# A two-layer decoder: first projections accumulated tile by tile, wide modulation rows moved into the first feed-forward

## The chip, the core and the metric

The kernel runs on one core of one Trainium2 chip. The core has TensorE (PE, matrix products), VectorE (DVE), ScalarE (ACT), GpSimd (POOL) and SyncE (SP), which here issues the loads and stores, and 16 DMA engines. The metric is the device time of one execution in microseconds (us), median of several runs. Lower is better.

## The reference

The reference is a decoder trunk of two layers for 1024 tokens of width 1024. A small vector `cond = silu(c)` is multiplied with a 1024 x 6144 matrix in each layer; the six parts of the result (48 columns of 128, called modulation) shift, scale and gate the two sub-layers.

```python
cond = jax.nn.silu(c)
for l in range(DEPTH):                                  # 2
    mod = cond @ w_mod[l] + b_mod[l]
    sh1, sc1, gt1, sh2, sc2, gt2 = [m[:, None, :] for m in jnp.split(mod, N_MOD, axis=-1)]
    h = rms_norm(x, norm_g[l, 0]) * (1.0 + sc1) + sh1
    y = mixer_block(h, positions, w_in[l], ...)         # conv | sparse attention | linear attention | gMLP, then w_o
    x = x + gt1 * rms_norm(y, norm_g[l, 1])
    h = rms_norm(x, norm_g[l, 2]) * (1.0 + sc2) + sh2
    y = jnp.square(jax.nn.relu(h @ w_up[l])) @ w_down[l]
    x = x + gt2 * rms_norm(y, norm_g[l, 3])
```

## The kernel before, in words

Activations lie transposed: a tile is 128 features x 512 tokens, eight tiles make 1024 features. The tokens go in two halves, `hf` 0 and 1. The program runs `mods_start`, then `mix(0,0)`, `mix(0,1)`, `ff(0,0)`, `mix(1,0)`, `ff(0,1)`, `mix(1,1)`, `ff(1,0)`, `ff(1,1)`. A scheduler that runs when the program is built interleaves them on each engine's queue, which is then fixed; between engines semaphores hold the order.

A product of float precision is made of three matmuls (`mm3`, L166 to L169): high part by high, high by low, low by high. So a GEMM for one 128-wide chunk of output (`gemm`, L171) is 8 tiles x 3 = 24 matmuls of 128x512. Its weights come in two halves of 256 KB: SP loads `raw_a` (L152), ScalarE casts the high part (L161), VectorE subtracts to get the low part (`sub`, L125). Lanes a, b and f are three sets of such weight buffers: a for the first and last projections of a mixer, b for the projections of linear attention, gMLP and convolution, f for the feed-forward. `h` tiles are made by `make_h` from x, the reciprocal norm R, the scale A1 and the shift, again as a high and a low part (two VectorE operations, L134, and one ScalarE operation, L203, for each tile).

A modulation column (`mod_col`, L228) takes 128 outputs: two loads of a 128x512 row of weights (256 KB each), for each a VectorE multiply with a sum along the row (L232, followed by a short read of the accumulator), and one short operation that adds the two sums and the bias. `mods_start` (L248) makes the columns of the first shift and scale, 32 rows named `mw`, in twelve buffers, together with the reciprocal norm; the h tiles follow. The other 80 columns, 160 rows named `mr`, have two buffers in the pool `work` (`mods`, L271). They are written in the program after the convolution of `mix(0,0)` (parts 2 to 4 of layer 0) and after `mix(0,1)` (part 5 of layer 0, all of layer 1), and the scheduler puts them between other VectorE work from early on.

In `mix(0,0)` the chunk for the gates (10) and the five for sparse attention (17 to 21) are projected first, each in a PSUM bank of the tag mm. Rotary tables (`rope_tables`) are made by VectorE from the positions, transposed and spread by small matmuls, copied by ScalarE, written to memory (`cosd`, `sind`) and read back as `cs`; GpSimd multiplies q and k with them. Then come key compression (L650), attention (L744 on), linear attention, gMLP and convolution, and the four groups' outputs are normalised, split (L216 on ScalarE, L125 on VectorE) and projected by `w_o` in lane a.

## Time and profile before

| | us |
|---|---|
| median of 3 runs | 2655.94 |
| lowest, highest | 2654.65, 2660.86 |
| span of the profiled execution | 2656.2 |
| TensorE busy in it | 2513.5 |
| VectorE busy in it | 1680.0 |
| ScalarE busy in it | 1310.3 |

The profile is of one execution; its span is within 0.3 us of the median of the runs. A busy time counts an engine's instructions from start to end; matmuls overlap, so the pitch from one start to the next tells more than a duration. The granted clock is a share of TensorE's full clock; its two levels here are 1.0 (2.4 GHz) and 0.5 (1.2 GHz). The rows that are read stand two sections below.

### The profile page before, as it was taken

To read this page: it belongs to the slowest core of one execution; us is meant where nothing else is said; L and a number is where in the kernel's file an instruction comes from. 1 tells how busy PE (TensorE), PEld (TensorE's weight loads), DVE (VectorE), ACT (ScalarE), POOL (GpSimd) and SP (SyncE) were. 2 spreads that over 40 slices of the span, in tenths; PEclk is the share of its full clock that TensorE was granted. 3 is DMA by queue.
4 is the path that set the end of the run, shared out by engine and by line. 5 is a ranking of instruction groups with operands and counts; after the bars stand their busy time and mean duration, and the time that the engine had idled before them with its cause. 6 is when DMAs were issued, how large, how long until landed. Compare 5 with 4: busy or idle time off the path is not lost.

```text
span 2656.2 us, 34273 instructions
## 1 busy us (share of the span) xinstructions
PE 2513.5 (95%) x11690; PEld 1989.3 (75%) x11690; DVE 1680.0 (63%) x3540; ACT 1310.3 (49%) x2649; POOL 56.5 (2%) x65
## 2 busy tenths in 40 slices
PE   2899879999999999999999999999999999999998
PEld 1676657677778887767788887777777888788887
DVE  7797987888574448457674446547876544534446
ACT  3474534468654345356653435345775443434343
POOL 0100000200000000010000000001000000000000
PEclk9999989999999999999999999999999999999999
DMA  7435566511343334222243334222123333533332
GB/s 270 138 97 174 192 204 202 179 53 36 100 142 98 96 99 143 82 71 69 95 144 100 96 97 145 88 61 89 40 76 121 98 96 99 179 97 98 96 99 84
DMA packets 168937, 301.56 MB, mean 114 GB/s; under 512 B 20453, under 2 KB 24122, under 8 KB 168762
## 3 DMA queue, kind: packets, MB, share of 16 engines
q1 hardware_dynamic: 168762, 299.37, 36.3%
q8 instruction: 92, 1.51, 0.2%
q14 instruction: 83, 0.68, 0.1%
HBM read 281.47 MB, written 17.83 MB: 113 GB/s over the span
## 4 chain that ended last, share of the span: by engine, by line
PE 76%; DVE 10%; ACT 4%; DMA 4%; issue 2%; POOL 0%; DVEq 0%; SPq 0%; ACTq 0%; POOLq 0%
PE ps_ff L168 16%; PE ps_ff L169 16%; PE ps_ff L167 16%; PE ps_mm L167 6%; PE ps_mm L169 6%; PE ps_mm L168 6%; DMA mr<-in_w_mod_dram 3%; PE ps_pv L705 1%; PE ps_pv L704 1%; DVE mr L232 1%; PE ps_mm L699 1%; ACT bp L754 1%; PE ps_t L189 1%; PE ps_s L744 1%; DVE w_a L125 1%
## 5 line engine op out<-in xcount | busy, mean ns | idle before, releaser
L161 ACT CAST w_f<-raw_f 128x512 fp32r<-128x512 f32 x504 | 313.3, 622 | 649.7 <-PE ps_ff L168 638.6
L125 DVE TENSOR_TENSOR w_f<-raw_f,w_f 128x512 fp32r<-128x512 f32 x504 | 348.7, 692 | 261.6 <-ACT w_f L161 254.7
L169 PE MATMUL ps_ff<-h,w_f 128*128 128x512 f32 x1024 | 405.9, 397 | 17.1 <-DVE w_f L125 17.1
L167 PE MATMUL ps_ff<-h,w_f 128*128 128x512 f32 x1024 | 404.8, 396 | 4.8 <-ACT h L203 4.8
L168 PE MATMUL ps_ff<-h,w_f 128*128 128x512 f32 x1024 | 406.6, 397 | 0.6 <-DVE h L134 0.4
L167 PE MATMUL ps_ff<-hid,w_f 128*128 128x512 f32 x992 | 388.9, 392 | 0.1
L168 PE MATMUL ps_ff<-hid,w_f 128*128 128x512 f32 x992 | 388.6, 392 | 0.0
L169 PE MATMUL ps_ff<-hid,w_f 128*128 128x512 f32 x992 | 388.2, 391 | 0.0
L167 PE MATMUL ps_mm<-h,w_a 128*128 128x512 f32 x832 | 336.4, 405 | 34.8 <-ACT w_a L161 30.5
L169 PE MATMUL ps_mm<-h,w_a 128*128 128x512 f32 x832 | 332.7, 400 | 11.7 <-DVE w_a L125 11.6
L168 PE MATMUL ps_mm<-h,w_a 128*128 128x512 f32 x832 | 338.8, 409 | 0.9 <-DVE h L125 0.9
L131 DVE TENSOR_TENSOR y<-y,ps_ff 128x512 f32<-128x512 f32 (+1 forms) x232 | 154.9, 668 | 238.0 <-PE ps_ff L169 237.1
L161 ACT CAST w_a<-raw_a 128x512 fp32r<-128x512 f32 x208 | 128.6, 618 | 233.0 <-PE ps_mm L168 216.2
L169 PEld LDWEIGHTS ps_ff<-h,w_f 128*128 128x128 f32 x1024 | 195.0, 190 | 60.1 <-DVE w_f L125 18.8
L125 DVE TENSOR_TENSOR w_a<-raw_a,w_a 128x512 fp32r<-128x512 f32 x208 | 143.3, 689 | 152.2 <-ACT w_a L161 146.0
L167 PEld LDWEIGHTS ps_ff<-h,w_f 128*128 128x128 f32 x1024 | 195.4, 191 | 47.6 <-ACT h L203 6.5
L168 PEld LDWEIGHTS ps_ff<-h,w_f 128*128 128x128 f32 x1024 | 195.0, 190 | 45.2 <-issue 2.7
L167 PEld LDWEIGHTS ps_mm<-h,w_a 128*128 128x128 f32 x832 | 158.0, 190 | 81.2 <-ACT w_a L161 33.6
L167 PEld LDWEIGHTS ps_ff<-hid,w_f 128*128 128x128 f32 x992 | 186.6, 188 | 40.5 <-issue 1.4
L168 PEld LDWEIGHTS ps_ff<-hid,w_f 128*128 128x128 f32 x992 | 186.7, 188 | 39.1 <-issue 1.0
L169 PEld LDWEIGHTS ps_ff<-hid,w_f 128*128 128x128 f32 x992 | 186.7, 188 | 37.8 <-issue 0.5
L169 PEld LDWEIGHTS ps_mm<-h,w_a 128*128 128x128 f32 x832 | 157.9, 190 | 55.8 <-DVE w_a L125 15.1
(350 smaller groups left out, 3586.4 us busy)
## 6 DMA issues: line engine op xcount, KB each, us to landing
raw_f<-in_w_up_dram SPq DMA_DIRECT2D x256, 256.0 KB, 2.7
raw_f<-in_w_down_dram SPq DMA_DIRECT2D x256, 256.0 KB, 2.6
mr<-in_w_mod_dram SPq DMA_DIRECT2D x160, 256.0 KB, 3.0
raw_a<-in_w_in_dram SPq DMA_DIRECT2D x144, 256.0 KB, 2.8
raw_a<-in_w_o_dram SPq DMA_DIRECT2D x64, 256.0 KB, 2.9
mw<-in_w_mod_dram SPq DMA_DIRECT2D x32, 256.0 KB, 4.4
bp<-in_cmp_w_dram SPq DMA_DIRECT2D x32, 256.0 KB, 4.6
raw_b<-in_w_in_dram SPq DMA_DIRECT2D x32, 256.0 KB, 3.0
```

Source lines behind the costliest of these rows:

```text
L125: V.tensor_tensor(out=out, in0=a, in1=b, op=ALU.subtract)
L131: eng.tensor_tensor(out=out, in0=a, in1=b, op=ALU.add)
L161: A.copy(hi, raw)
L167: PE.matmul(ps_ap, wh, xh, start=start, stop=False)
L168: PE.matmul(ps_ap, wh, xl, start=False, stop=False)
L169: PE.matmul(ps_ap, wl, xh, start=False, stop=stop)
L189: PE.matmul(p, ones, acc, start=True, stop=True)
L232: V.tensor_tensor_reduce(out=raw, in0=raw, in1=cond[kh], scale=1.0, scalar=0.0, op0=ALU.mult, op1=ALU.add, accum_out=mp[:, kh:kh + 1])
L699: PE.transpose(tp[0:kn, hh, :], cols(h0 + hh), ident)
L704: PE.matmul(pv[:, h0:h0 + nh, :], vst, th[0:kn], start=first[0], stop=False)
L705: PE.matmul(pv[:, h0:h0 + nh, :], vst, tl[0:kn], start=False, stop=last)
L744: PE.matmul(sp[:, 0:w], qh[:, h0 + hh, :], KX[:, 128 * k0:128 * k0 + w], start=True, stop=False)
```

## The change

`cond` becomes one tile of 1024, and a modulation row is 1024 wide: one load of 512 KB and one VectorE operation for a column instead of two. The start makes columns, h tiles and the six chunks' GEMMs together: after tile k of h, each of the six chunks gets its three matmuls of that tile, in six PSUM banks (two each of the tags mm, ff and s); their weights are loaded and split for four tiles at a time, at k = 0 and k = 4. `gate_part` and `nsa_part` take these banks as they are. The modulation of parts 2 to 4 of layer 0 (24 rows) runs after the convolution with three buffers in the place of the convolution's tiles. Part 5 of layer 0 and all of layer 1 but one part (48 rows) are handed out one row for each down-projection unit of `ff(0,0)`, with two buffers; the last part (8 rows) in `ff(0,1)`. The table matmuls of `rope_tables` move from the tag s to the single bank of the tag t.

```diff
-    def mod_col(l, j, k, mk):
-        mp = work.tile([128, 2], F32, name="mp", tag="mp", bufs=4)
-        for kh in range(2):
-            raw = mk(w_mod[l, 8 * j + k, :, kh * T:kh * T + T], [128, T])
-            V.tensor_tensor_reduce(out=raw, in0=raw, in1=cond[kh], scale=1.0, scalar=0.0,
-                                   op0=ALU.mult, op1=ALU.add, accum_out=mp[:, kh:kh + 1])
-        stt(par[l]["mod"][:, j, k:k + 1], mp[:, 0:1], mp[:, 1:2], par[l]["bmod"][:, 8 * j + k:8 * j + k + 1],
-            ALU.add, ALU.add)
+    def mod_dot(l, j, k, mk, acc):
+        raw = mk(w_mod[l, 8 * j + k], [128, 1024])
+        V.tensor_tensor_reduce(out=raw, in0=raw, in1=cond, scale=1.0, scalar=0.0,
+                               op0=ALU.mult, op1=ALU.add, accum_out=acc)
...
-    def mods_start():
-        with region("su") as su:
+    EARLY = (10, 17, 18, 19, 20, 21)
+
+    def start():
+        d = par[0]
+        early = {}
+        with region("kw", "right") as kw, region("su") as su:
             def mk(src, shape):
-                t = su.tile(shape, F32, name="mw", tag="mw", bufs=12)
+                t = su.tile(shape, F32, name="mw", tag="mw", bufs=5)
                 dma(out=t, in_=src)
                 return t
+
+            def wload(n, kh):
+                raw = kw.tile([128, 4, 128], F32, name="raw_k", tag="raw_k", bufs=6)
+                dma(out=raw, in_=w_in[0, n, :, 4 * kh:4 * kh + 4, :])
+                return raw
+
+            def wsplit(raw):
+                hi, lo = (kw.tile([128, 4, 128], F32R, name="w_k", tag="w_k", bufs=12) for _ in range(2))
+                A.copy(hi, raw)
+                sub(lo, raw, hi.bitcast(F32))
+                return hi, lo
...
             for k in range(8):
+                ma = work.tile([128, 2, 1], F32, name="ma", tag="ma", bufs=4)
                 for j in (0, 1):
-                    mod_col(0, j, k, mk)
+                    mod_dot(0, j, k, mk, ma[:, j, :])
+                add(d["mod"][:, 0:2, k:k + 1], ma, bm[:, 0:2, k:k + 1])
                 mod_scale(0, 1, slice(k, k + 1))
+                if k % 4 == 0:
+                    raws = [wload(n, k // 4) for n in EARLY]
+                h = make_h(xt, R, d["A1"], d["mod"][:, 0, :], (k,))
+                hs = h if k == 0 else hs + h
+                if k % 4 == 0:
+                    ws = {n: wsplit(r) for n, r in zip(EARLY, raws)}
+                for i, n in enumerate(EARLY):
+                    if k == 0:
+                        early[n] = ps(("mm", "mm", "ff", "ff", "s", "s")[i])
+                    hi, lo = ws[n]
+                    mm3(early[n], hi[:, k % 4, :], lo[:, k % 4, :], hs[k][0], hs[k][1], k == 0, k == 7)
...
-    def mods(l, js):
+    def mods(l, j, pl, bufs):
 
         def mk(src, shape):
-            t = work.tile(shape, F32, name="mr", tag="mr", bufs=2)
+            t = pl.tile(shape, F32, name="mr", tag="mr", bufs=bufs)
...
+        ma = work.tile([128, 8], F32, name="mv", tag="mv", bufs=2)
+        for k in range(8):
+            mod_dot(l, j, k, mk, ma[:, k:k + 1])
+            if k == 7:
+                add(par[l]["mod"][:, j, :], ma, par[l]["bmod"][:, 8 * j:8 * j + 8])
+                mod_scale(l, j, slice(0, 8))
+            yield
...
                 for w, dst in ((0, cosd), (128, sind)):
-                    p = ps("s")
+                    p = ps("t")
...
-                    mods(0, (2, 3, 4))
+                    with region("md", "right") as rg:
+                        for _ in mods_all(((0, 2), (0, 3), (0, 4)), rg, 3):
+                            pass
...
+                next(filler, None)
                 for k in range(G):
...
-    mods(0, (5,))
-    mods(1, range(6))
-    xt = ff(0, 0)
+    xt = ff(0, 0, ((0, 5), (1, 1), (1, 0), (1, 2), (1, 4), (1, 3)))
...
-    xt = ff(0, 1)
+    xt = ff(0, 1, ((1, 5),))
```

On TensorE, the first matmuls of the program in the kernel before (`ps_mm_417` is the bank of chunk 10, `h_346` and `h_347` the high and low part of the first h tile, `h_352` and `h_353` the second's):

```order
L189 MATMUL ps_t_194<-nt_171,ones_71 128x512
L167 MATMUL ps_mm_417<-h_346,w_a_420 128x512
L168 MATMUL ps_mm_417<-h_347,w_a_420 128x512
L169 MATMUL ps_mm_417<-h_346,w_a_422 128x512
L167 MATMUL ps_mm_417<-h_352,w_a_420 128x512
L168 MATMUL ps_mm_417<-h_353,w_a_420 128x512
```

And of the change, the end of the first h tile's round and the begin of the second's (`h_224`, `h_225` are the first tile's parts, `h_287`, `h_288` the second's):

```order
L167 MATMUL ps_s_272<-h_224,w_k_248 128x512
L168 MATMUL ps_s_272<-h_224,w_k_248 128x512
L169 MATMUL ps_s_272<-h_224,w_k_249 128x512
L167 MATMUL ps_mm_252<-h_287,w_k_228 128x512
L167 MATMUL ps_mm_256<-h_287,w_k_232 128x512
L167 MATMUL ps_ff_260<-h_287,w_k_236 128x512
L167 MATMUL ps_ff_264<-h_287,w_k_240 128x512
L167 MATMUL ps_s_268<-h_287,w_k_244 128x512
L168 MATMUL ps_mm_252<-h_288,w_k_228 128x512
L169 MATMUL ps_mm_252<-h_287,w_k_229 128x512
```

Before, one chunk ran through all eight tiles in one bank; now all six banks take a tile's matmuls before the next tile.

On VectorE, where the normalised outputs of `mix(0,0)` are split for the output projection (`of_2341` and `of_2463` are the convolution's outputs), the kernel before:

```order
L134 SCALAR_TENSOR_TENSOR of_2341<-of_2341,gain0_99,nt_2512 128x512
L134 SCALAR_TENSOR_TENSOR of_2463<-of_2463,gain0_99,nt_2512 128x512
L131 TENSOR_TENSOR nt_2717<-nt_2717,nt_2719 128x512
L125 TENSOR_TENSOR h_2730<-of_2341,h_2729 128x512
L134 SCALAR_TENSOR_TENSOR mod0_100<-mp_6417,bmod0_96 128x1
L125 TENSOR_TENSOR h_2734<-of_2463,h_2733 128x512
L232 ISA mr_6426,mp_6425<-mr_6426,cond0_125 128x512
L232 ISA mp_6425 128x1
L125 TENSOR_TENSOR h_2738<-of_2160,h_2737 128x512
L232 ISA mr_6429,mp_6425<-mr_6429,cond1_126 128x512
```

The same place in the change (`of_2280` and `of_2402` are the convolution's outputs):

```order
L134 SCALAR_TENSOR_TENSOR of_2280<-of_2280,gain0_99,nt_2451 128x512
L134 SCALAR_TENSOR_TENSOR of_2402<-of_2402,gain0_99,nt_2451 128x512
L232 ISA mr_2471,mv_2461<-mr_2471,cond_125 128x1024
L232 ISA mv_2461 128x1
L232 ISA mr_2474,mv_2461<-mr_2474,cond_125 128x1024
L232 ISA mv_2461 128x1
L232 ISA mr_2477,mv_2461<-mr_2477,cond_125 128x1024
L232 ISA mv_2461 128x1
L131 TENSOR_TENSOR nt_2546<-nt_2546,nt_2548 128x512
L125 TENSOR_TENSOR h_2559<-of_2280,h_2558 128x512
L232 ISA mr_2480,mv_2461<-mr_2480,cond_125 128x1024
L232 ISA mv_2461 128x1
```

Between the convolution's last operation and the projection's fifth weight split 23 of the 24 wide rows of parts 2 to 4 now stand, 17 of them ahead of the last split of the outputs; before, six narrow rows stood there.

On SP, loads in `ff(0,0)` in the change (before, this stretch holds `raw_f` loads and those of `w_o` and x alone):

```order
L305 DMA mr_6525<-in_w_mod_dram 128x1024
L305 DMA mr_6549<-in_w_mod_dram 128x1024
L152 DMA raw_f_7386<-in_w_up_dram 128x512
L152 DMA raw_f_7404<-in_w_up_dram 128x512
L410 DMA bg_9470<-in_gmlp_b_dram 64x128
L305 DMA mr_6573<-in_w_mod_dram 128x1024
L305 DMA mr_6597<-in_w_mod_dram 128x1024
L152 DMA raw_f_7430<-in_w_up_dram 128x512
L152 DMA raw_f_7448<-in_w_up_dram 128x512
L305 DMA mr_6800<-in_w_mod_dram 128x1024
```

Wide rows and weight halves alternate in one queue.

## Rows read from the trace of the kernel before

**Rows 1.** From the page, part 1: busy us (share of the span) and instructions.

```profile
PE 2513.5 (95%) x11690; PEld 1989.3 (75%) x11690; DVE 1680.0 (63%) x3540; ACT 1310.3 (49%) x2649; POOL 56.5 (2%) x65
```

**Rows 2.** Table of windows: span, busy us of each engine, clock, DMA share, GB/s.

```profile
25.00:50.00 25.00, 1.02 (x3) 0.79 (x3) 24.50 (x73) 5.56 (x8) 0.00 (x0) 1.00 0.66 212
100.00:275.00 175.00, 164.84 (x882) 122.91 (x879) 151.32 (x455) 97.44 (x249) 4.75 (x8) 0.98 0.41 126
350.00:375.00 25.00, 16.93 (x45) 10.84 (x45) 22.72 (x51) 10.64 (x17) 0.00 (x0) 0.78 0.54 168
400.00:550.00 150.00, 137.28 (x724) 102.61 (x723) 122.49 (x310) 64.67 (x135) 13.86 (x13) 0.99 0.56 176
850.00:950.00 100.00, 100.00 (x443) 82.84 (x442) 41.71 (x63) 41.04 (x68) 0.00 (x0) 1.00 0.34 98
1020.00:1350.00 330.00, 318.71 (x1538) 246.91 (x1537) 211.65 (x466) 181.49 (x399) 12.55 (x13) 0.97 0.28 88
```

**Rows 3.** Timeline of VectorE, start to 49 us: start, duration, engine, line, operation.

```profile
14.12 0.68 DVE L232 CUSTOM_DVE_ANT_0 mw<-mw,cond 128x512 f32<-128x512 f32 x1
...
40.06 0.68 DVE L232 CUSTOM_DVE_ANT_0 mw<-mw,cond 128x512 f32<-128x512 f32 x1
40.67 0.08 DVE L232 DVE_READ_ACCUMULATOR2_ANT mp<- 128x1 f32 x1
...
47.48 1.41 DVE L134 SCALAR_TENSOR_TENSOR h<-nt,mod,h 128x512 fp32r<-128x512 f32 x2
```

**Rows 4.** Timeline of TensorE, first six GEMMs.

```profile
50.42 0.63 PE L167 MATMUL ps_mm<-h,w_a 128*128 128x512 f32 x1
50.85 0.63 PE L168 MATMUL ps_mm<-h,w_a 128*128 128x512 f32 x1
...
54.10 0.39 PE L167 MATMUL ps_mm<-h,w_a 128*128 128x512 f32 x1
54.33 0.39 PE L168 MATMUL ps_mm<-h,w_a 128*128 128x512 f32 x1
...
93.39 0.40 PE L169 MATMUL ps_mm<-h,w_a 128*128 128x512 f32 x1
```

**Rows 5.** Timeline of TensorE, ScalarE and GpSimd, rotary tables to first attention.

```profile
60.25 0.60 PE L322 MATMUL ps_t<-ident,sc 128*17 128x128 f32 x4
...
67.11 0.59 ACT L329 COPY o<-ps_s 128x512 f32<-128x512 f32 x1 [0.27 <-PE ps_s L327]
...
75.97 2.56 POOL L128 TENSOR_TENSOR p<-p,cs 128x512 f32<-128x512 f32 x2 [72.89 <-DMA raw_b<-in_w_in_dram]
...
96.04 1.50 POOL L128 TENSOR_TENSOR p<-p,cs 128x512 f32<-128x512 f32 x1
...
109.14 0.33 PE L744 MATMUL ps_s<-KS,qh 128*128 128x128 f32 x1
```

**Rows 6.** Answer for the tile mr (160 modulation rows 512 wide).

```profile
L275 SPq DMA_DIRECT2D mr<-in_w_mod_dram x160: 327/328/1397, 73.6 to 540.7; - x160
L232 DVE CUSTOM_DVE_ANT_0 mr<-mr,cond x160: 647/686/1200, 82.2 to 544.5; 128x512 f32<-128x512 f32 x160
...
  DMA mr<-in_w_mod_dram: 36.6, 49
...
DMA to landing us min/median/max: 2.4/3.0/5.7
```

**Rows 7.** TensorE, convolution's end to output projection: timeline.

```profile
272.24 0.39 PE L169 MATMUL ps_mm<-h,w_b 128*128 128x512 f32 x1
...
281.46 0.80 PE L167 MATMUL ps_mm<-h,w_a 128*128 128x512 f32 x1 [3.36 <-ACT h L216]
```

**Rows 8.** Groups of instructions by line, 272 to 290 us.

```profile
L167 PE MATMUL ps_mm<-h,w_a 128*128 128x512 f32 x7 | 3.5, 502 | 3.6 <-ACT h L216 3.4 <-ACT w_a L161 0.3
L168 PE MATMUL ps_mm<-h,w_a 128*128 128x512 f32 x5 | 3.3, 664 | 0.9 <-DVE h L125 0.9
L169 PE MATMUL ps_mm<-h,w_a 128*128 128x512 f32 x5 | 2.4, 482 | 0.0
```

More of the change, by code (lines that the diff above doesn't have):

```diff
@@ L195, in rstd, with make_h @@
         return R
-    def make_h(xt, R, Ac, shc):
+    def make_h(xt, R, Ac, shc, ks=range(8)):
         h = []
-        for k in range(8):
+        for k in ks:
             t = nt()
@@ L244, in mod_scale @@
             mul(d["G1" if j == 2 else "G2"][:, ks], m, d["ng"][:, 1 if j == 2 else 3, ks])
-    cond = [const.tile([128, T], F32, name=f"cond{hf}") for hf in range(2)]
-    def mods_start():
-        with region("su") as su:
+    EARLY = (10, 17, 18, 19, 20, 21)
[3 more added lines that the diff above has]
+        with region("kw", "right") as kw, region("su") as su:
             def mk(src, shape):
-                t = su.tile(shape, F32, name="mw", tag="mw", bufs=12)
+                t = su.tile(shape, F32, name="mw", tag="mw", bufs=5)
                 dma(out=t, in_=src)
                 return t
+            def wload(n, kh):
[7 more added lines that the diff above has]
+                return hi, lo
             for hf in range(2):
+                cs = slice(hf * T, hf * T + T)
                 t1, t2 = (su.tile([128, T], F32, name="ct", tag="ct", bufs=4) for _ in range(2))
-                dma(out=cond[hf], in_=c[:, hf * T:hf * T + T].to_broadcast([128, T]))
-                logsig(t2, cond[hf], t1)
+                dma(out=cond[:, cs], in_=c[:, cs].to_broadcast([128, T]))
+                logsig(t2, cond[:, cs], t1)
                 A.activation(t2, t2, AF.Exp)
-                mul(cond[hf], cond[hf], t2)
+                mul(cond[:, cs], cond[:, cs], t2)
             xt = load_x(0)
@@ L410, in gmlp_part, with gate_part @@
         return group_out(y, st_[1], d["gain"][:, 6:8])
-    def gate_part(l, hf, h, gr, rg, lane):
-        p = ps("mm")
-        gemm(p, lane, w_in[l, GLA0], h)
+    def gate_part(l, hf, h, gr, rg, lane, early={}):
+        p = early.get(GLA0)
+        if p is None:
+            p = ps("mm")
+            gemm(p, lane, w_in[l, GLA0], h)
         lrT = rg.tile([32, T], F32, name="lrT")
@@ L566, in gla_part, with nsa_part @@
         return group_out(y, st_[1], d["gain"][:, 4:6])
-    def nsa_part(l, hf, h, rg, gates):
+    def nsa_part(l, hf, h, rg, gates, early={}):
         d = par[l]
@@ L581, in inproj @@
         def inproj(k):
-            p = ps("mm")
-            gemm(p, "a", w_in[l, NSA0 + k], h)
+            p = early.get(NSA0 + k)
+            if p is None:
+                p = ps("mm")
+                gemm(p, "a", w_in[l, NSA0 + k], h)
             return p
@@ L826, in ytile, with norm, mix @@
         return work.tile([128, T], F32, name="y", tag="y", bufs=8)
-    def norm(l, hf, xt, R=None):
+    def norm(l, hf, xt):
         d = par[l]
-        if R is None:
-            R = rms_R(xt, 1.0 / 1024)
+        R = rms_R(xt, 1.0 / 1024)
         return make_h(xt, R, d["A1"], d["mod"][:, 0, :])
-    def mix(l, hf, h, between=None):
+    def mix(l, hf, h, between=None, early={}):
         d = par[l]
@@ L842, in mix @@
                     with region("gl", "right") as rg:
[L843 removed]
+                        gates, lrT = gate_part(l, hf, h, gr, rg, "a", early)
                         rope_tables()
[L845 removed]
+                        yn = nsa_part(l, hf, h, es.enter_context(region("ns")), gates, early)
                         ol = gla_part(l, hf, h, rg, "b", sx, lrT)
@@ L881, in mix, with ff, ff_body @@
         return res
-    def ff(l, hf):
+    def ff(l, hf, todo=()):
+        with region("md") as rg:
+            return ff_body(l, hf, mods_all(todo, rg, 2))
+    def ff_body(l, hf, filler):
         d = par[l]
@@ L959, in load_x @@
         return xt
-    xt, R0 = mods_start()
-    h = norm(0, 0, xt, R0)
+    h, early = start()
     xt = load_x(1)
-    h = mix(0, 0, h, lambda: norm(0, 1, xt))
+    h = mix(0, 0, h, lambda: norm(0, 1, xt), early)
     mix(0, 1, h)
-    mods(0, (5,))
-    mods(1, range(6))
-    xt = ff(0, 0)
+    xt = ff(0, 0, ((0, 5), (1, 1), (1, 0), (1, 2), (1, 4), (1, 3)))
     h = norm(1, 0, xt)
     mix(1, 0, h)
-    xt = ff(0, 1)
+    xt = ff(0, 1, ((1, 5),))
     h = norm(1, 1, xt)
```

14 lines of the change are left out of this document (7 added, 7 removed).

## The prediction

> **What bounds the kernel now.** I read the page first. TensorE is busy 95% of the span, VectorE 63%, ScalarE 49% [rows 1]. So the span is the matmuls plus the places where TensorE waits or runs at half clock, and only those places can move. The table of windows shows where they are [rows 2]. From 25 to 50 us TensorE works 1.02 us while VectorE works 24.50 of 25: VectorE sets the start. From 100 to 275 TensorE is idle 10.2 us, from 350 to 375 it is idle 8.1 us at a mean granted clock of 0.78, from 400 to 550 it is idle 12.7 us. In a feed-forward stretch (850 to 950) it is idle 0 us, with VectorE at 41.7% and the DMA engines at 34%. From 1020 to 1350, where layer 1's first mixer is interleaved with feed-forward work and no modulation runs, it is idle 11.3 us in 330.
>
> The timeline then tells what the start is made of. VectorE runs the 32 modulation rows from 14.12 to 40.7 at a pitch of 0.61 us (40.06 to 40.67), with the h tiles among and after them; the last h is done at 48.89 [rows 3]. TensorE starts its first six GEMMs (144 matmuls) at 48.98, at half clock (0.43 us each, 50.42 to 50.85) and at full clock (0.23 us each) from 54.10 [rows 4]. They end at 93.8 [rows 4], and rotary tables, gates and weight splits all run underneath.
>
> **The start, part by part.** The change feeds the same 144 matmuls tile by tile, so they run under VectorE's work. VectorE's own list changes thus: 16 rows of 1024 at an estimated 1.15 us (a 512 row's 0.61 twice would be 1.22; one fixed part falls away) instead of 32 x 0.61: 18.4 for 19.5, -1.1; 8 short adds instead of 16, about -1; 12 weight subtracts put ahead of the end, at the same pitch since they have the same 128x512 shape, 12 x 0.61 = +7.3. So the last h comes about 5 us later, near 54, and the last 18 matmuls (4.1 us) end near 59. TensorE has 18 x 0.23 = 4.1 us of work for each 4.7 us of VectorE, so it never holds VectorE up. The DMA adds 3 MB of weights to a stretch with a third of its time free [rows 2]: no cost taken, at most 3 us. Alone this is 93.8 - 59 = 35 us of lead.
>
> Most of that lead can't be used. In the order of the change, the next long work on TensorE (compression, attention, the first lane-b GEMM) stands behind the rotary tables, and these no longer have GEMMs to hide under: the position load stands in SP's queue behind the loads of the second half's x, which wait for the start's last scratch tile; the gates' transposes stand behind all 144 matmuls; the table sines come after the gates on VectorE; and four table matmuls now share one PSUM bank. Before, the first table transpose ran at 60.25 and the last table copy ended at 67.70, 7.5 us [rows 5]. Now the transposes can start near 61, and the one bank makes the same steps take about 9: 70. Written to memory and read back, two transfers of 2.4 to 3.0 us [rows 6]: 76. That is just where GpSimd's first rotary multiply ran before, at 75.97 [rows 5]. But before, GpSimd's last multiply began at 96.04, because it waited for q's GEMMs; now all inputs are there, and six multiplies of 1.28 to 1.50 take 8.5 us: end near 84.5 instead of 97.5. The first attention matmul followed that end by 11.6 us (97.5 to 109.14 [rows 5]): compression adds, 64 compression matmuls. So it comes at 96: **-13 us**. Bounds: -25 if TensorE finds enough lane-b work to move ahead, -3 if the tables take 10 us longer.
>
> **The rows of (0,2) to (0,4).** Before, 160 rows of 512 wide sat between other VectorE work from 82 to 545 us, and VectorE stood still before 49 of them for 36.6 us on their transfers [rows 6]. 48 of these leave the stretch from 100 to 272; TensorE's idle time there, 10.2 us, mostly waits for softmax steps. Taken: **-4**, bounds 0 and -10.
>
> They come back as 24 wide rows between the convolution and the output projection. There TensorE's last convolution matmul starts at 272.24, the first of the output projection at 281.46, and in 272 to 290 only 7 + 5 + 5 = 17 GEMM matmuls run, 3.9 us of work at full clock: 14 us lost already [rows 7, 8]. VectorE now has 17 of the 24 rows before the last split of the normalised outputs, and SP issues the fifth weight half of the projection behind the 23rd row's load, which waits for a free buffer. By VectorE's own list: 24 x 1.15 + about 24 other operations x 0.61 = 42 us. By the three buffers: (1.15 + 0.33 for the issue + landing) / 3 for each row. A transfer of 256 KB lands in 2.4 to 5.7 us, 3.0 at the median [rows 6]; 512 KB is not in the trace. I take the second half at 0.7 to 1 us on top, so 3.1 to 6.5, likeliest 4, since the median is the nearest row: 1.83 x 24 = 44 us. Meanwhile TensorE has two and a half GEMMs, 60 matmuls, 13.6 us. Loss 28 to 30 instead of 14: **+14**. Bounds: +10, if the first rows start under the last GEMM; +35 at a landing of 6.5.
>
> The Trainium skill prices such a load on "DMA: Bandwidth & Descriptors", section "Anatomy of one DMA", at about 2.0 us plus bytes over 436 GB/s, measured on GpSimd's queue: 2.6 us for 256 KB, near the 3.0 here, and an estimate of 3.2 for 512 KB. By it the buffers would not bind, the sum would be some 5 us lower, and the rows in the feed-forward below would be free.
>
> **The other 56 columns.** Their 112 narrow rows leave 275 to 545. In 350 to 375 idle time and half clock cost about 12 us, in which 10 rows ran; I take **-8** (bounds -4, -12). In 400 to 550 the idle 12.7 us would be 5.1 at the rate of 1020 to 1350 [rows 2], so **-8** (bounds -3, -12). The wait near 343 stays: VectorE's row there is residual work.
>
> 48 of them run as wide rows inside ff(0,0), the last 8 in ff(0,1). A unit of 12 matmuls lasts 2.73 us; VectorE's work for it is one subtract, one add and a row, 0.61 + 0.61 + 1.15 = 2.37. It fits, but with two buffers a row can come only every (1.15 + 0.33 + landing) / 2: 2.74 us at a landing of 4. That is the unit's own pace. VectorE, waiting for a row, has the next weight subtracts queued behind it, and SP, waiting for a buffer, has the next weights. What softens it: the rows come in groups of eight with up-projections between, and weights are a few units ahead. Taken: **+3**, bounds 0 and +25.
>
> **Sum.** -13 - 4 + 14 - 8 - 8 + 3 = -16 against the span of 2656.2, which is 0.3 us from the median of the runs: **2640 us**.
>
> **The rivals.**
> *More of the lead kept* (2.5 in 10). TensorE takes lane-b GEMMs, output-projection work or the second half's norm while the tables are made, and the rows' loads land in 3 us: -25 - 6 + 10 - 10 - 10 + 0 = -41, 2615. For: transfers of 256 KB landed in 2.4 at best. Against: the order places the first lane-b GEMM behind attention's first matmuls.
> *Nothing left* (2 in 10). The tables take 10 us longer (start -3) and the rest stays: -6, 2650. This is also the case where the change does less than it says: the matmuls move, what waits behind them doesn't.
> *Slower: the long loads* (1.5 in 10). One mechanism, the landing of a 512 KB row behind few buffers. At 5 us a row comes every 2.16 us from three buffers, 24 x 2.16 = 52, +24 instead of +14; and every 3.24 us from two, 0.51 beyond the unit, 48 x 0.51 = 24 instead of 3. Total -16 + 10 + 21 = +15, 2671. It decides from a landing of about 4.8 up. For: 256 KB took up to 5.7, and SP feeds the weights through the same queue. Against: the median of 3.0.
> *Slower: half clock in the start* (0.5 in 10). If the 144 matmuls, going round six PSUM banks with a pause at each tile, never left half clock, they would take 144 x 0.43 = 62 us from about 21: 83 instead of 59, everything behind them 24 us later: +8, 2664. The Trainium skill has such a rule in "TensorE: Matmul & The Clock Gate", section "A second HAM failure mode: psum-queue depth-cycling": matmuls that cycle through banks, with small idle times between the groups, made the clock oscillate. The traces so far speak against it: at half clock 18 matmuls need 7.7 us for each 4.7 of VectorE, so TensorE would be busy without pause, and busy without pause it left half clock at 54.10 [rows 4]; and from 100 to 275, with many short waits and changing banks, the granted clock was 0.98 [rows 2].
>
> **How the numbers follow.** The forecast has 3.5 chances in 10, with its own range 2628 to 2650; the rivals have the 6.5 given. A measurement of this kernel can tell about 0.3%, 8 us. Faster by more (below 2648): the forecast, most of the kept lead, a part of "nothing left": 0.63. Within 8 us: 0.19. Slower: the two last rivals and the upper bounds (+35 at the projection): 0.18. The range runs from a little below the second case to the slower one: 2605 to 2671.
>
> **What will show it.** Early matmuls should end near 59 at full clock; the first attention matmul should start near 96 (over 105: the tables are longer; under 88: lead kept). The output projection should begin to flow some 28 us after the convolution's last matmul; under 18 the term is wrong. The wide rows' landing is in the list of DMA issues: 4 us is mine, 5 and more the slow rival. In ff(0,0) TensorE should wait under 5 us for weight subtracts. I am wrong at the root if narrow rows cost more TensorE time than their idle windows show, or if the scheduler's order hides the 24 rows better than the list of VectorE tells.

## The result

The changed kernel takes 2675.93 us (median of 4 runs, 2675.12 to 2677.22) against 2656.58 for the kernel before in the same comparison: a ratio of 1.0073, with a 95% interval of 1.0059 to 1.0087. It is 19 us slower. The prediction said 2640 us, 16 us faster, and a range up to 2671.

The page of the kernel after, its busy times and the loads of modulation rows (KB each, median us to landing):

```profile
PE 2533.9 (95%) x11690; PEld 1997.4 (75%) x11690; DVE 1660.2 (62%) x3270; ACT 1313.0 (49%) x2649; POOL 54.2 (2%) x65
...
mr<-in_w_mod_dram SPq DMA_DIRECT2D x80, 512.0 KB, 4.3
...
mw<-in_w_mod_dram SPq DMA_DIRECT2D x16, 512.0 KB, 7.5
```

TensorE is busy for 20 us more than in [rows 1] with the same matmuls; VectorE for 20 us less. A load of 512 KB lands in 4.3 us at the median; in the start, where five are under way and the first projection's weights besides, in 7.5.

The stretches of [rows 2] and some more in the kernel after (columns as there):

```profile
25.00:50.00 25.00, 23.63 (x96) 18.37 (x96) 24.23 (x49) 7.13 (x11) 0.00 (x0) 1.00 0.82 276
50.00:105.00 55.00, 35.31 (x151) 23.65 (x149) 30.28 (x90) 14.70 (x30) 7.82 (x6) 0.69 0.41 131
75.00:100.00 25.00, 12.41 (x49) 9.11 (x50) 15.37 (x34) 6.80 (x14) 7.82 (x6) 0.51 0.18 56
100.00:275.00 175.00, 160.03 (x854) 120.75 (x851) 117.51 (x318) 99.44 (x252) 4.81 (x8) 0.97 0.20 62
350.00:375.00 25.00, 15.06 (x46) 10.36 (x45) 20.94 (x33) 11.10 (x19) 0.00 (x0) 0.75 0.53 173
400.00:550.00 150.00, 144.41 (x756) 109.48 (x755) 85.79 (x171) 67.21 (x137) 12.54 (x13) 0.99 0.27 82
780.00:920.00 140.00, 131.60 (x551) 103.79 (x549) 108.38 (x187) 48.89 (x81) 0.64 (x1) 0.98 0.82 266
```

From 25 to 50 us TensorE now works 23.63 us where it worked 1.02; its matmuls start every 0.43 us (half clock) until 27.7 us and every 0.23 us (full clock) from there, which the row's clock of 1.00 passes over. From 50 to 105 it is idle for 19.7 us and its mean granted clock is 0.69; from 75 to 100 it is idle for 12.6 us, at 0.51. From 400 to 550 its idle time is 5.6 instead of 12.7 us. From 780 to 920, inside ff(0,0), where it never stood still before, it is idle for 8.4 us, with the DMA engines at 82%.

The span alone does not tell which of these decide. So I took the same matmul in two traces and subtracted its starts. Each column is one matmul of the program: the first of attention, the last GEMM matmul of the convolution, the sum for the second half's norm behind the first output projection (336.17 us in the kernel before), GEMM matmuls of the feed-forwards that started at the times given in the kernel before, and the program's last sum (2645.79 us). Numbers are us against the kernel before, minus is earlier:

| kernel | attention 109.14 | convolution's end 272.24 | norm 336.17 | 558.41 | 790.24 | 1000.04 | 1450.14 | last 2645.79 |
|---|---|---|---|---|---|---|---|---|
| after | -4.9 | -4.0 | +13.3 | -3.6 | -4.0 | +11.7 | +16.7 | +18.5 |
| e_early | +1.2 | +6.4 | +4.3 | +4.6 | +2.5 | +2.5 | +1.5 | +1.2 |
| e_mods | +0.1 | +2.1 | +20.6 | +3.6 | +3.2 | +15.6 | +18.3 | +19.7 |
| e_ropemid | -11.7 | -10.4 | +7.6 | -8.3 | -8.6 | +6.7 | +9.1 | +9.0 |
| e_nest | -5.7 | -2.7 | +3.0 | -13.2 | -13.5 | -1.8 | -0.6 | +0.2 |
| e_md6 | -4.9 | -3.6 | +13.1 | -2.9 | -3.2 | +10.4 | +12.8 | +14.1 |
| e_ff4 | -2.8 | -1.8 | +16.9 | +0.9 | +0.5 | +32.0 | +34.3 | +34.5 |
| c_nr | -11.3 | -7.8 | -1.9 | -18.0 | -18.4 | -3.5 | -1.5 | -1.3 |
| c_mixn | -11.5 | -7.3 | -2.3 | -10.3 | +9.2 | +9.3 | +8.7 | +8.7 |
| x_1_0 | -11.5 | -7.6 | -1.6 | -18.0 | -18.6 | -8.8 | -6.1 | -4.7 |
| x_4_3b | -13.3 | -9.9 | -4.2 | -20.3 | -20.8 | -15.5 | -15.2 | -13.7 |

The table tells where time goes, and the ratios below tell how much a kernel takes: each row is one execution, all are set against one trace of the kernel before, and that kernel had a median of 2656.6 us in the comparison with the change but of 2651.3 to 2653.2 in those of the experiments. So an experiment's last column can lie up to 8 us under what its ratio gives (e_early: +1.2, and a ratio worth 9 us). What is read here are the first columns and the differences between neighbouring columns of a row.

The row "after" reads as three places. The start's lead is 4.9 us at the first attention matmul and 4.0 at the convolution's end. Between there and the norm 17.3 us are lost. By 558 us 16.9 are won back. Then ff(0,0) loses 15.7, and ff(0,1) 4.4 around its eight rows (+12.3 for a matmul at 1370 us of the kernel before, +16.7 at 1450).

**The start.** Timeline of TensorE after, from the last early matmul to the first of attention (L463 gates, L359 and L364 rotary tables, L489 linear attention's sums, L691 compression, L785 attention), and three of GpSimd's rotary products, the first and the last among them:

```profile
61.23 0.39 PE L169 MATMUL ps_s<-h,w_k 128*128 128x512 f32 x1
61.55 0.46 PE L463 MATMUL ps_t<-ident,nt 64*128 64x64 f32 x4
64.02 0.60 PE L359 MATMUL ps_t<-ident,sc 128*17 128x128 f32 x4 [2.02 <-DVE sc L354]
65.28 2.07 PE L364 MATMUL ps_t<-st,sl 17*128 17x512 f32 x2 [0.67 <-ACT st L361]
68.03 2.07 PE L364 MATMUL ps_t<-st,sl 17*128 17x512 f32 x2 [0.68 <-ACT o L366]
...
75.22 2.07 PE L364 MATMUL ps_t<-st,sl 17*128 17x512 f32 x2 [0.68 <-ACT o L366]
...
91.96 2.04 PE L489 MATMUL ps_ff<-tri,g 128*128 128x128 f32 x8 [5.52 <-DVE g L134]
94.90 9.37 PE L691 MATMUL ps_mm<-bp,zc 128*32 128x128 f32 x64 [0.90 <-DVE zc L131]
104.20 0.33 PE L785 MATMUL ps_s<-KS,qh 128*128 128x128 f32 x1
...
81.19 1.26 POOL L128 TENSOR_TENSOR p<-p,cs 128x512 f32<-128x512 f32 x1 [78.11 <-DMA cs<-cosd]
...
86.58 1.54 POOL L128 TENSOR_TENSOR p<-qs,cs 128x512 f32<-128x512 f32 x1 [2.66 <-PE ps_t L663]
...
91.29 1.26 POOL L128 TENSOR_TENSOR p<-qs,cs 128x512 f32<-128x512 f32 x1 [0.62 <-DVE qr L131]
```

The 144 matmuls end at 61.6, 32 us earlier than in [rows 4]. Then TensorE has 43 us in which only small groups like these run, one at a time, nearly each after a wait. The pairs of L364 take 2.07 us with a wait for ScalarE's copy between; the tables run from 64.02 to 77.92 with the last copy. Before they took 7.5 us [rows 5].

**Convolution to output projection.** Timeline of TensorE after, and groups of instructions from 268 to 286 us:

```profile
268.29 0.39 PE L169 MATMUL ps_mm<-h,w_b 128*128 128x512 f32 x1
...
275.64 0.80 PE L167 MATMUL ps_mm<-h,w_a 128*128 128x512 f32 x1 [3.26 <-ACT h L216]
...
292.71 0.79 PE L168 MATMUL ps_mm<-h,w_a 128*128 128x512 f32 x1 [6.45 <-DVE h L125]
...
L232 DVE CUSTOM_DVE_ANT_0 mr<-mr,cond 128x1024 f32<-128x1024 f32 x9 | 10.9, 1221 | 1.2 <-DMA mr<-in_w_mod_dram 1.2
L168 PE MATMUL ps_mm<-h,w_a 128*128 128x512 f32 x3 | 2.4, 813 | 0.8 <-DVE h L125 0.8
...
L167 PE MATMUL ps_mm<-h,w_a 128*128 128x512 f32 x4 | 2.2, 552 | 3.3 <-ACT h L216 3.3
```

Against [rows 7, 8]: in 18 us 10 of the projection's matmuls ran instead of 17 (four of L167 and three of L168 in these groups, three of L169 in the timeline), while VectorE took nine wide rows (10.9 us) and three of the eight splits. The wait of 6.45 us ends with VectorE's split of an output (L125).

**The first feed-forward.** The tile mr after, 740 to 1000 us (count, duration in ns, first and last start; idle time of VectorE before it, times; us to landing):

```profile
L232 DVE CUSTOM_DVE_ANT_0 mr<-mr,cond x48: 1218/1225/1228, 783.0 to 918.2; 128x1024 f32<-128x1024 f32 x48
...
  DMA mr<-in_w_mod_dram: 30.9, 38
...
DMA to landing us min/median/max: 3.5/4.3/5.6
```

48 rows in 135 us, one each 2.88 us; VectorE stood before 38 of them, for 30.9 us. TensorE's longest waits there, from 780 to 920 us (us in total, times, longest):

```profile
PE ps_ff L167 <- DVE y L131: 6.4, 4, 2.9
PE ps_ff L169 <- DVE w_f L125: 0.7, 1, 0.7
```

Four times a down-projection's first matmul waits for VectorE's add to y, which frees its bank; weight subtracts, which the prediction had in mind, hold TensorE up for 0.7 us. Two stretches of 20 us show what follows (columns as in the table above):

```profile
820.00:840.00 20.00, 15.94 (x59) 11.53 (x59) 14.22 (x26) 4.23 (x7) 0.00 (x0) 0.91 0.78 252
...
880.00:900.00 20.00, 18.50 (x72) 14.39 (x73) 16.64 (x30) 3.73 (x6) 0.00 (x0) 0.91 0.83 270
```

The granted clock fell to 0.91 in these two, behind such waits; in the other five from 780 to 920 it was 1.00. The loss is not spread evenly over the rows: by the same subtraction of starts, the shift goes from -3.3 to +3.7 us between the matmuls at 823.8 and 840.1 us of the kernel before, and from +4.8 to +11.1 between those at 867.3 and 889.1; that is 13.3 of the 15.7.

### The profile page after: what moved, and what is told of

Its sections match the earlier page's. It is cut to its first block, busy times and chain, and to the rows that moved or that the text cites. A ratio compares the mean times of both kernels' runs of the same rounds, so it can differ in the third digit from the quotient of the medians.

```text
span 2674.7 us, 33893 instructions
## 1 busy us (share of the span) xinstructions
PE 2533.9 (95%) x11690; PEld 1997.4 (75%) x11690; DVE 1660.2 (62%) x3270; ACT 1313.0 (49%) x2649; POOL 54.2 (2%) x65
## 4 chain that ended last, share of the span: by engine, by line
PE 66%; DVE 5%; DMA 4%; ACT 3%; issue 2%; POOL 0%; SPq 0%; DVEq 0%; ACTq 0%; POOLq 0%
PE ps_ff L167 14%; PE ps_ff L169 14%; PE ps_ff L168 14%; PE ps_mm L167 5%; PE ps_mm L169 5%; PE ps_mm L168 5%; DMA mr<-in_w_mod_dram 3%; PE ps_pv L746 1%; PE ps_mm L740 1%; PE ps_pv L745 1%; ACT bp L795 1%; DVE y L131 1%; PE ps_t L189 1%; PE ps_s L785 1%; PE ps_mm L691 1%
## 5 line engine op out<-in xcount | busy, mean ns | idle before, releaser
L125 DVE TENSOR_TENSOR w_f<-raw_f,w_f 128x512 fp32r<-128x512 f32 x504 | 348.2, 692 | 229.3 <-ACT w_f L161 218.1
L169 PE MATMUL ps_ff<-h,w_f 128*128 128x512 f32 x1024 | 404.7, 396 | 16.3 <-DVE w_f L125 16.3
L167 PE MATMUL ps_ff<-h,w_f 128*128 128x512 f32 x1024 | 403.0, 394 | 3.3 <-ACT h L203 3.2
L168 PE MATMUL ps_ff<-h,w_f 128*128 128x512 f32 x1024 | 404.8, 396 | 0.1
L167 PE MATMUL ps_ff<-hid,w_f 128*128 128x512 f32 x992 | 392.0, 395 | 9.6 <-DVE y L131 8.2
L168 PE MATMUL ps_ff<-hid,w_f 128*128 128x512 f32 x992 | 390.1, 393 | 0.3 <-DVE hid L125 0.3
L169 PE MATMUL ps_ff<-hid,w_f 128*128 128x512 f32 x992 | 389.7, 393 | 0.0
L168 PE MATMUL ps_mm<-h,w_a 128*128 128x512 f32 x784 | 321.3, 411 | 9.6 <-DVE h L125 9.5
L169 PE MATMUL ps_mm<-h,w_a 128*128 128x512 f32 x784 | 314.6, 402 | 8.9 <-DVE w_a L125 8.9
L167 PE MATMUL ps_mm<-h,w_a 128*128 128x512 f32 x784 | 318.6, 407 | 4.2 <-ACT h L216 3.3
L125 DVE TENSOR_TENSOR w_a<-raw_a,w_a 128x512 fp32r<-128x512 f32 x196 | 135.2, 690 | 175.5 <-ACT w_a L161 170.1
L169 PEld LDWEIGHTS ps_ff<-h,w_f 128*128 128x128 f32 x1024 | 194.4, 190 | 60.1 <-DVE w_f L125 18.6
L167 PEld LDWEIGHTS ps_ff<-hid,w_f 128*128 128x128 f32 x992 | 187.2, 189 | 56.1 <-DVE y L131 6.8
L167 PEld LDWEIGHTS ps_ff<-h,w_f 128*128 128x128 f32 x1024 | 194.1, 190 | 45.9 <-ACT h L203 5.1
L161 ACT CAST w_a<-raw_a 128x512 fp32r<-128x512 f32 x196 | 121.5, 620 | 215.7 <-PE ps_mm L168 208.5
L168 PEld LDWEIGHTS ps_ff<-h,w_f 128*128 128x128 f32 x1024 | 194.2, 190 | 43.1 <-issue 2.4
L168 PEld LDWEIGHTS ps_ff<-hid,w_f 128*128 128x128 f32 x992 | 187.6, 189 | 39.7 <-DVE hid L125 1.6
L169 PEld LDWEIGHTS ps_ff<-hid,w_f 128*128 128x128 f32 x992 | 187.5, 189 | 39.3 <-DVE w_f L125 0.7
L168 PEld LDWEIGHTS ps_mm<-h,w_a 128*128 128x128 f32 x784 | 149.4, 191 | 53.3 <-DVE h L125 13.7
L169 PEld LDWEIGHTS ps_mm<-h,w_a 128*128 128x128 f32 x784 | 149.6, 191 | 49.5 <-DVE w_a L125 11.1
```

What stands on the lines that cost most here:

```text
L125: V.tensor_tensor(out=out, in0=a, in1=b, op=ALU.subtract)
L161: A.copy(hi, raw)
L167: PE.matmul(ps_ap, wh, xh, start=start, stop=False)
L168: PE.matmul(ps_ap, wh, xl, start=False, stop=False)
L169: PE.matmul(ps_ap, wl, xh, start=False, stop=stop)
```

## The experiments

Theory 1 was that three places decide, each by its own mechanism: in the start the chain of gates, tables and rotary products that lost its cover; behind the convolution the 24 rows that stand on VectorE ahead of splits; in the feed-forward the rows' buffers, which pace the loads while VectorE waits in front of other work. The rivals are in the expectations.

**e_early: the start alone.** The change's `start()`; the 80 later columns again as narrow rows in their old places.

```diff
-                    with region("md", "right") as rg:
-                        for _ in mods_all(((0, 2), (0, 3), (0, 4)), rg, 3):
-                            pass
+                    mods_n(0, (2, 3, 4))        # 512 wide, two buffers, as before
...
+    mods_n(0, (5,))
+    mods_n(1, range(6))
-    xt = ff(0, 0, ((0, 5), (1, 1), (1, 0), (1, 2), (1, 4), (1, 3)))
+    xt = ff(0, 0)
```

> The start of the change alone: tile-by-tile GEMMs of six chunks and wide rows in the start; all later modulation is as before (160 rows of 512, two buffers, in the same places). Theory 1 (the lead of the start is mostly eaten by the chain of gates, rotary tables, rotary products and compression behind it): the end of the convolution comes 2 to 6 us earlier than before, total 2650 to 2655. Rival (the lead is good and is lost only to what the moved rows do): 10 us or more earlier at the convolution's end, total 2640 to 2646.

Measured: ratio 1.0035 (1.0022 to 1.0049). Neither: the lead is not small but gone, with the convolution's end 6.4 us later. TensorE's wait for the compression sums, and VectorE's group of narrow rows from 76 to 104 us:

```profile
100.61 3.62 PE L712 MATMUL ps_mm<-bp,zc 128*32 128x128 f32 x16 [8.32 <-DVE zc L131]
...
L305 DVE CUSTOM_DVE_ANT_0 mr<-mr,cond 128x512 f32<-128x512 f32 x2 | 1.4, 692 | 6.4 <-DMA mr<-in_w_mod_dram 6.4
```

Two narrow rows that were put into this chain made VectorE stand for 6.4 us on their loads; the compression adds are behind them. In the kernel before GEMMs ran under such waits. So the chain, not the GEMMs, sets the time from 62 to 104 us, and these 6.4 us count nearly in full: the first attention matmul comes 6.1 us later than in the change.

**e_mods: the moved rows alone.** The start, its narrow rows and the table matmuls' banks as before; all else as in the change.

> The moved and widened modulation alone: start, first GEMMs and rotary tables as before; 24 wide rows behind the convolution, 48 in the first feed-forward, 8 in the second. Theory 1 (the places cost by themselves): +14 to +16 between convolution and output projection, -13 until 550 us, +14 to +16 in ff(0,0), +5 in ff(0,1), so 2672 to 2680. Rival (the cost needs the new start, for instance through its buffers and banks): 2650 to 2660.

Measured: ratio 1.0098 (1.0083 to 1.0113), 26 us. By the table +18.5 behind the convolution, -17.0 by 558, +12.4 in ff(0,0). Theory 1 holds: the places cost without the new start. It also shows that taking 48 narrow rows out of the stretch before the convolution's end won nothing there by itself (+2.1). With the new start it may have won something: between attention and the convolution's end e_early, with the narrow rows there, loses 5.2 us, and the change, without them, 0.9. Why the two halves of the change give +6.4 and +2.1 at the convolution's end and both together -4.0 stays open; the orders on TensorE differ between the three.

**e_ropemid: tables inside the start.** `rope_tables()` is called after the fifth h tile, so that its matmuls stand among the early ones; four buffers for the start's rows and fewer for the tables, for room.

```diff
+                if k == 4:
+                    rope_tables()
...
                         gates, lrT = gate_part(l, hf, h, gr, rg, "a", early)
-                        rope_tables()
```

> The whole change with the rotary tables made inside the start, after the fifth h tile, so that their matmuls stand among the early ones; four instead of five buffers for the start's rows. Theory 1 (the tables behind the start hold up rotary products and attention): the first attention matmul comes 10 to 16 us earlier than with the change as it is (104 us), and the convolution's end 6 to 12 earlier: total 2664 to 2670. Rival (the GEMMs of lane b set the convolution's end, attention has slack): attention earlier, the convolution's end within 3 us, total 2673 to 2677.

Measured: ratio 1.0054 (1.0039 to 1.0069) where the change has 1.0073 (1.0059 to 1.0087); the intervals overlap, so the starts are read and not the totals. TensorE, the tables' matmuls now at full clock among the others (1.12 us for a pair), and the first of attention:

```profile
62.12 1.12 PE L366 MATMUL ps_t<-st,sl 17*128 17x512 f32 x2
...
64.29 1.12 PE L366 MATMUL ps_t<-st,sl 17*128 17x512 f32 x2
...
97.47 0.33 PE L787 MATMUL ps_s<-KS,qh 128*128 128x128 f32 x1
```

Attention comes 6.8 us earlier than in the change, the convolution's end 6.4: less than the 10 to 16 of theory 1, but carried over whole, so the rival (attention has slack) falls. Of what is missing I know one part: the reading back of the tables was issued at 67.9 us and landed 6.1 us later, and GpSimd's first product started only at 74.14. The chain of rotary products and compression adds follows as before; I did not take it apart.

**e_nest: the 24 rows under the convolution's GEMMs.** Their three buffers lie in the room of the gMLP's tiles, free as soon as that is done.

```diff
-                    with region("cv", "right") as rg, region("gm", "right") as rg2:
-                        og = gmlp_part(l, hf, h, rg2, "b", sx)
-                        oc = conv_part(l, hf, h, rg, "b", sx)
-                    with region("md", "right") as rg:
-                        for _ in mods_all(((0, 2), (0, 3), (0, 4)), rg, 3):
-                            pass
+                    with region("cv", "right") as rg:
+                        with region("gm", "right") as rg2:
+                            og = gmlp_part(l, hf, h, rg2, "b", sx)
+                        with region("md", "right") as rg3:
+                            oc = conv_part(l, hf, h, rg, "b", sx)
+                            for _ in mods_all(((0, 2), (0, 3), (0, 4)), rg3, 3):
+                                pass
```

> The whole change, but the 24 wide rows of parts 2 to 4 stand in the room of the gMLP's tiles as soon as these are done, with the same three buffers, so that they run under the convolution's GEMMs instead of behind them. Theory 1 (their place between the convolution and the output projection costs, since 23 of them stand ahead of the splits and weights that TensorE waits for): the 16 us lost there fall to under 5, total 10 to 14 us under the change's. Rival (they cost wherever they run in this mixer, by VectorE's time or the DMA engines): the convolution's end moves later by 8 us or more and the total by under 4.

Measured: ratio 1.0032 (1.0021 to 1.0044), 11 us under the change's by the ratios. From the convolution's end to the norm 5.7 us are lost instead of 17.3 (theory 1 had said under 5), and the convolution's end is only 1.3 us later than in the change. Theory 1 holds: it was the place.

**e_md6: more buffers in the old place.** Six instead of three: `mods_all(((0, 2), (0, 3), (0, 4)), rg, 6)`.

> The whole change with six instead of three buffers for the 24 wide rows behind the convolution. Theory 1 (VectorE's own list of rows and splits takes that long; VectorE waited for only 4 us on rows there): the loss between convolution and output projection stays at 12 to 18 us. Rival (the rows are paced by their buffers, as in the prediction's second bound): it falls below 8.

Measured, one run: 2671.99 us, where the kernel before has 2653.23 (a ratio of 1.007, as the change); +16.7 between convolution and norm, as in the change (+17.3). TensorE's longest waits from 262 to 312 us (us in total, times, longest), of e_md6 and, by its side, of the change from 268 to 300:

```profile
PE ps_mm L168 <- DVE h L125: 8.7, 5, 6.8
...
PE ps_mm L168 <- DVE h L125: 9.3, 3, 6.4
```

With twice the buffers VectorE does not wait for a row there at all in the list of its waits, and TensorE waits for the same splits as long. VectorE's list is the limit, as theory 1 says.

**e_ff4: four buffers in the feed-forward.** `mods_all(todo, rg, 4)` instead of 2.

> The whole change with four instead of two buffers for the wide rows inside ff(0,0) and ff(0,1). Theory 1 (a row is paced by its buffer: (1.2 + 0.3 + 4.3) / 2 = 2.9 us against a unit's 2.73, and VectorE stands in front of weight subtracts meanwhile): waits of VectorE on rows fall from 31 us to under 8, ff(0,0) loses under 4 us instead of 16, total 2656 to 2663. Rival (VectorE's load or the DMA engines' share is the limit): waits stay, total 2672 to 2677.

Measured: ratio 1.0139 (1.0122 to 1.0156), worse than the change. SP's queue, TensorE's longest wait from 780 to 920 us and the tile mr from 740 to 1000:

```profile
783.52 15.47 SPq L305 DMA_DIRECT2D mr<-in_w_mod_dram  x11
...
PE ps_ff L167 <- ACT w_f L161: 19.5, 1, 19.5
...
L232 DVE CUSTOM_DVE_ANT_0 mr<-mr,cond x48: 1214/1220/1227, 787.8 to 889.5; 128x1024 f32<-128x1024 f32 x48
...
  DMA mr<-in_w_mod_dram: 11.0, 17
```

Eleven row loads stand in one block ahead of the next weights, and TensorE waits 19.5 us for weights once. The loss comes at one spot: the shift is +0.5 us at 790.24 and +29.5 at 801.8 already. Behind the block the rows run at 2.2 us each and VectorE waits 11.0 us instead of 30.9. So the run doesn't decide the question: the wait was shorter, and a second mechanism, the order in SP's queue, hid what that was worth. I take the block to come from the room for the rows, which becomes free only when the units of the first groups are past, so that their rows are a backlog with an older place in the program than the weights; x_4_3b below tries that.

**c_nr: both repairs** (e_ropemid and e_nest), the feed-forward as in the change.

> Both repairs: rotary tables inside the start and the 24 rows under the convolution's GEMMs; the rows in the feed-forward as in the change. If the parts add up: ratio of the change 1.0073, less 5 us for the tables and 12 for the rows: 0.999 to 1.002 of the kernel before. Rival (each repair only moves the wait on to the next, as the start did): 1.004 or more.

Measured: ratio 1.0017 (1.0007 to 1.0026). The repairs nearly add up: -18.0 at 558 us where the change has -3.6. ff(0,0) then takes 14.9 of it.

**c_mixn: the 56 columns in the second mixer.** As c_nr, with 112 narrow rows between the first output projection and the feed-forward, none in the feed-forwards.

> Both repairs, and the other 56 columns as 112 narrow rows with two buffers from the output projection of the first half until the first feed-forward runs alone, none in the feed-forwards. Theory 1 (in the feed-forward a row costs about 0.33 us, in the second mixer the narrow ones cost 13 us in all): the 17 to 20 us of the feed-forwards are gone, 10 to 13 come back before 550 us, ratio 0.995 to 0.999. Rival (rows cost as much in the second mixer once they are crowded there): 1.000 to 1.005.

Measured: ratio 1.0057 (1.0041 to 1.0074). The rival is right: between 558 and 790 us 19.5 are lost, with no single long wait. The tile mr there, 540 to 700 us:

```profile
L307 DVE CUSTOM_DVE_ANT_0 mr<-mr,cond x45: 660/684/692, 541.6 to 674.0; 128x512 f32<-128x512 f32 x45
...
  DMA mr<-in_w_mod_dram: 1.4, 2
```

VectorE waited for 1.4 us only, so it is hardly the rows' loads. That leaves the rows' work among attention's small operations; this is argued and not shown.

**x_4_3b: four buffers and no backlog.** As c_nr, with four buffers, and the rows handed out only from the fourth of the eight groups on.

```diff
-            return ff_body(l, hf, mods_all(todo, rg, 2))
+            return ff_body(l, hf, mods_all(todo, rg, 4))
...
-                next(filler, None)
+                for _ in range((g >= 3) * (1 + (n < 2))):
+                    next(filler, None)
```

> Both repairs (rotary tables inside the start, 24 rows under the convolution), and the rows of the first feed-forward with four buffers, handed out only from the fourth of the eight groups on, so that no backlog of rows stands ahead of the weights in SP's queue (with four buffers alone 11 row loads stood in a row there). Theory 1 (a row costs TensorE time only where VectorE waits for its load, or where its load stands ahead of weights): VectorE's waits on rows fall from 31 us to under 8, the feed-forwards lose under 4 us, ratio 0.994 to 0.998. Rival (VectorE's 1.2 us for each row, or the DMA engines' share, is what costs): the loss in the feed-forwards stays above 10 us, ratio 1.000 to 1.003.

**x_1_0: one buffer.** As c_nr, with `mods_all(todo, rg, 1)`.

> Both repairs, and the rows of the first feed-forward with one buffer instead of two: each load waits for the row before, (1.2 + 0.3 + 4.3) = 5.9 us for a row, so 48 rows take some 280 us, thinly spread. Theory 1 (crowding: rows that come as fast as a unit's pace leave VectorE no room behind a wait): single waits stay, but far apart, the loss in ff(0,0) falls from 15 to 3 to 8 us. Rival (each wait of VectorE costs TensorE about a third of its length wherever it stands): more waiting with one buffer, loss above 15 us, ratio 1.002 or more.

Measured: x_4_3b has a ratio of 0.9972 (0.9962 to 0.9983), x_1_0 of 0.9991 (0.9982 to 1.0000). The tile mr from 740 to 1100 us, of c_nr with two buffers, of x_1_0 with one, of x_4_3b with four:

```profile
L232 DVE CUSTOM_DVE_ANT_0 mr<-mr,cond x48: 1215/1225/1228, 768.5 to 903.0; 128x1024 f32<-128x1024 f32 x48
...
  DMA mr<-in_w_mod_dram: 30.5, 37
...
L232 DVE CUSTOM_DVE_ANT_0 mr<-mr,cond x48: 1224/1225/1229, 768.6 to 998.9; 128x1024 f32<-128x1024 f32 x48
...
  DMA mr<-in_w_mod_dram: 68.8, 48
...
L232 DVE CUSTOM_DVE_ANT_0 mr<-mr,cond x48: 1209/1220/1227, 767.1 to 877.1; 128x1024 f32<-128x1024 f32 x48
...
  DMA mr<-in_w_mod_dram: 12.4, 15
```

Two buffers: 30.5 us of waiting, 14.9 us lost in ff(0,0) by the table. One buffer: 68.8 us of waiting but over 230 us instead of 135, 9.8 lost. Four: 12.4 us of waiting, 5.3 lost. On SP at most two row loads stand together in x_4_3b, where e_ff4 had eleven. x_4_3b lies in theory 1's range of ratios, with waits and a loss somewhat above what theory 1 said; x_1_0's loss lies between the two theories. The stretches in which the rows run, of c_nr, x_1_0 and x_4_3b (columns as in [rows 2]):

```profile
767.00:905.00 138.00, 129.22 (x544) 102.92 (x543) 107.07 (x188) 48.30 (x80) 0.64 (x1) 0.98 0.81 267
...
767.00:1000.00 233.00, 225.64 (x985) 183.81 (x984) 151.28 (x252) 87.27 (x144) 0.94 (x1) 1.00 0.61 201
...
767.00:877.00 110.00, 106.40 (x464) 86.11 (x463) 97.90 (x171) 38.93 (x64) 0.00 (x0) 1.00 0.89 315
```

With four buffers VectorE is busier (89% of the stretch where c_nr has 78%) and so are the DMA engines (0.89 and 0.81), and yet less is lost: the rival, that VectorE's work or the DMA engines' share is the price, falls. With less waiting for loads TensorE is idle for 3.6 us instead of 8.8. x_4_3b changes the number of buffers and the place of the rows together, and the share of each is not shown. VectorE's waiting is not the measure of the loss either: with one buffer it is more than twice as long, and less is lost. TensorE's idle time is then 7.4 us, hardly less than in c_nr, but its granted clock stays at 1.00, where in c_nr it fell to 0.91 in two stretches of 20 us (800 to 820, 860 to 880), some 3.6 us by an estimate from 0.09 of these 40 us. Of the 5.1 us between the two losses 1.4 are idle time; most of the rest fits the clock. x_4_3b is 0.3% faster than the kernel before, by 7 us, and so faster than both kernels.

## Why the prediction was wrong

By its steps, against the row "after" of the table:

| step | predicted | measured |
|---|---|---|
| start, to the first attention matmul | -13 | -4.9 |
| narrow rows out of 100 to 272 | -4 | +0.9 |
| 24 rows behind the convolution | +14 | +17.3 |
| 350 to 550, narrow rows gone | -16 | -16.9 |
| 558 to 790 | 0 | -0.4 |
| rows in ff(0,0) | +3 | +15.7 |
| rows in ff(0,1) and all behind | 0 | +6.8 |
| sum | -16 | +18.5 |

**Right.** The 24 rows behind the convolution by VectorE's own list (42 us), not by their buffers: e_md6 and e_nest show both halves of that. The gain from 350 to 550, in its sum: by 375 us of the kernel before 4.3 us were back (predicted 8), behind it 12.6 (predicted 8), so two errors cancelled there. That the lead of the start would mostly go to what stands behind it.

**The start, mis-sized by 8 us.** The early matmuls ended at 61.6 (predicted 59) and the mechanism was right, but the step "the one bank makes the same steps take about 9" took 13.9. I had put the table matmuls in at the durations they had among GEMMs. Alone behind waits they run at half clock: 2.07 us for a pair here, 1.12 among the early matmuls in e_ropemid, which is 3.8 us for the four pairs; the mean granted clock from 50 to 105 us was 0.69. Then GpSimd's products took from 81.19 to 92.55, 11.4 us and not 8.5: it stands idle for 3.5 us among them, 2.66 of these before a product that waits, by the profile, for small matmuls on TensorE (L663). That is 5 and 3 of the 8 us. Two more errors cancel: the early matmuls ended 2.6 us late, and writing and reading back the tables took 3.3 us instead of 6.

The half clock was a rival of mine in the wrong place. Of the early matmuls themselves, which go round six banks, the trace shows a granted clock of 1.00 from 25 to 50 us, and from 27.7 us to the last of them 0.23 us from one start to the next wherever they follow each other directly. The rule that I had weighed (the Trainium skill, "TensorE: Matmul & The Clock Gate", section "A second HAM failure mode: psum-queue depth-cycling") did not come true there. The clock fell behind them: it was 0.51 from 75 to 100 us, where TensorE was idle for 12.6 of 25 us.

**100 to 272, wrong in sign.** I charged -4 for the rows that leave and nothing for what the new start does to this stretch. e_early, with the rows still there, loses 5.2 us in it. e_mods removes the same rows with the old start and gets nothing. By the prediction's own sentence TensorE's waits there are mostly for softmax steps, and a bound of 0 was too good.

**The first feed-forward, mis-sized by 13 us: the largest miss.** No single step made the sign: had this one cost the 3 us charged, the change would still be some 6 us slower. The formula gave the rows' pace rightly, and its input was wrong. A row each (1.15 + 0.33 + landing) / 2: at the 4.3 us that 512 KB took it gives 2.9, and the trace has 2.88. I had taken 4.0, which came out at 2.74, just the unit's 2.73, and then charged 3 us with bounds of 0 and 25. On such an edge the value between the bounds should not have been one next to the good one: 0.15 us for each of 48 rows is 7 us, less than half of the 15.7, so the pace alone is not the price. Seen from TensorE, 8.4 us of it are idle time (780 to 920), and the two drops of the clock are some 3.6 us, an estimate from 0.09 of two stretches of 20 us; the last 4 are not accounted for. The step that failed is that a row at the unit's own pace costs next to nothing: VectorE, late by its waits, held back the adds to y that free TensorE's banks, and not the weight subtracts that the prediction named. I also thought of the rows as lying in the down-projections alone, with pauses; they came one for every unit, in 135 us. The slow rival, "the long loads", had the mechanism of this term and its total (2671) lies 5 us from the result, but I gave it 1.5 chances in 10 and a landing of 5 us; behind the convolution it was wrong, since buffers did not bind there.

The Trainium skill's price for such a load ("DMA: Bandwidth & Descriptors", section "Anatomy of one DMA"), an estimate of 3.2 us, made for GpSimd's queue, is below every row here: the fastest of the 48 took 3.5 us, the median 4.3. By it the term would have been 0.

**ff(0,1) was not charged at all.** Its eight rows cost 4.4 us: VectorE stood 5.9 us before six of them, and TensorE again waited for adds to y (1.8 us in all). The other 2.4 us of that line of the table I did not look for.
